# Roll of an 8192 x 8192 matrix by 100 columns: the heads' DMAs moved from GpSimd to SP and ACT

## The chip, the cores and the metric

The kernel runs on one core of one Trainium2 chip. The metric is the device time in microseconds (us). Before the change the median of 3 runs is 816.8 us (815.75 to 818.27). Nothing is multiplied here: the kernel moves data, and its work is done by the core's 16 DMA engines, which are fed by queues that SP, ACT and GpSimd (POOL in the profile) issue to. VectorE (DVE) makes a few small copies.

## The reference

```python
def setup_inputs():
    return {"x": np.random.randn(8192, 8192).astype(np.float32), "shift": 100}

def reference(x, shift):
    return np.roll(x, shift, axis=1)
```

Every row of 8192 floats (32 KB) is turned to the right by s = 100 floats: `out[r, c] = x[r, c - 100]`, and the last 100 floats of a row come to its front. All of x, 268.44 MB, must be read, and as much written.

## The kernel before

Each output row is cut at column a. `a` is 100 rounded up to 128 and then raised by another 128, so a = 256, and g = a - s = 156.

**The long pieces** are columns 256 to 8191 of each output row: 7936 floats, 31,744 bytes, copied from DRAM to DRAM. The rows are taken in 128 blocks of 64. A block is four DMAs (j = 0 to 3) of 16 rows each; SP issues j = 0 and 2, ACT j = 1 and 3, all in line 43. Each of the DMAs is 496 KB and puts one row on each of the 16 DMA engines. In the last four blocks every DMA is cut into two halves of 248 KB. The semaphores that the framework gives to DMAs of SP and ACT are eight, taken in turn, and a DMA waits until the last user of its semaphore has landed. So at most eight DMAs of SP and ACT together are under way. In the kernel before SP has four of the eight semaphores for itself and ACT the other four.

**The heads** are columns 0 to 255 of each output row (1 KB). They are made of two runs of the input: the last 100 floats of the row and its first 156. They go through SBUF, in 16 stages of 512 rows, four rows to a partition (Q = 4). A stage has

- line 72: one DMA that reads, for three of every four rows, the 256 floats that straddle the end of one row and the beginning of the next, into tile `t` (384 KB in runs of 1 KB)
- line 73: the last 100 floats of each fourth row, into `h` (50 KB in runs of 400 bytes), and line 76: the first 156 floats of each first row, into `h` (78 KB in runs of 624 bytes)
- lines 74 and 77: two VectorE copies from `t` to `h`, which swap the order of the two runs
- line 80: one DMA that stores `h` (512 KB, runs of 1 KB) into columns 0 to 255 of the 512 output rows

All 64 of these DMAs are issued by GpSimd: first the 48 loads of the 16 stages, then the 16 stores. Both pools have 16 buffers, so that no stage waits for a buffer. GpSimd's DMAs have eight semaphores of their own. SP and ACT never wait for the heads, and the heads never wait for the long pieces: they meet on the DMA engines alone, and GpSimd's loop over the stages is traced after the loop of the long pieces but runs beside it from the start.

Of the kernel before, what the change touches and what calls it, by code (L numbers as in the profile page):

```python
# [1 line left out]

# [4 lines left out]


@with_exitstack
def kernel(  # L10
    ctx: ExitStack,
    tc: tile.TileContext,
    x: bass.AP,
    shift: int,
    out: bass.AP,
):
    nc = tc.nc
    n_rows, n_cols = x.shape
    s = shift % n_cols
    a = -(-s // 128) * 128  # L20
    if 0 < a <= 384 and a + 128 <= n_cols:
        a += 128
    g = a - s
    P = nc.NUM_PARTITIONS
    engines = [nc.sync, nc.scalar]
    n_chunks = 16
    rows = n_rows // n_chunks

    xm = x.rearrange("(c e j) w -> c j e w", e=16, j=4)
    om = out.rearrange("(c e j) w -> c j e w", e=16, j=4)
    if a < n_cols:
        blocks = n_rows // 64
        mid = (a + n_cols) // 256 * 128
        for c in range(blocks):
            parts = ((a, mid), (mid, n_cols)) if c >= blocks - 4 and a < mid else ((a, n_cols),)  # L40
            for j in range(4):
                for lo, hi in parts:
                    engines[j % 2].dma_start(out=om[c, j, :, lo:hi], in_=xm[c, j, :, lo - s:hi - s])
    if a == 0:
        return


    if a > 512:
        for i in range(n_chunks):
            r = slice(i * rows, (i + 1) * rows)  # L50
            nc.gpsimd.dma_start(out=out[r, :s], in_=x[r, n_cols - s:])
            if g > 0:
                nc.gpsimd.dma_start(out=out[r, s:a], in_=x[r, :g])
        return

    Q = 4  # L60
    n_st = n_rows // (P * Q)
    reads = ctx.enter_context(tc.tile_pool(name="reads", bufs=n_st))
    heads = ctx.enter_context(tc.tile_pool(name="heads", bufs=n_st))
    xt = x.rearrange("(k p q) c -> k p q c", q=Q, p=P)
    ot = out.rearrange("(k p q) c -> k p q c", q=Q, p=P)
    tiles = []
    for k in range(n_st):
        t = reads.tile([P, Q - 1, a], x.dtype)
        h = heads.tile([P, Q, a], x.dtype)
        lead = bass.AP(tensor=x.tensor, offset=(k * P * Q + 1) * n_cols - s,  # L70
                       ap=[[Q * n_cols, P], [n_cols, Q - 1], [1, a]])
        nc.gpsimd.dma_start(out=t[:], in_=lead)  # L72
        nc.gpsimd.dma_start(out=h[:, Q - 1, :s], in_=xt[k, :, Q - 1, n_cols - s:])  # L73
        nc.vector.tensor_copy(h[:, :Q - 1, :s], t[:, :, :s])  # L74
        if g > 0:
            nc.gpsimd.dma_start(out=h[:, 0, s:], in_=xt[k, :, 0, :g])  # L76
            nc.vector.tensor_copy(h[:, 1:, s:], t[:, :, s:])  # L77
        tiles.append(h)
    for k, h in enumerate(tiles):
        nc.gpsimd.dma_start(out=ot[k, :, :, :a], in_=h[:])  # L80


# [1 line left out]
_INS = ['x', 'shift']  # L84
_OUTS = [((8192, 8192), 'float32')]

_NUMBERS = {'shift': 100}


# [26 lines left out]
```

## Time and profile before

| what | value |
|---|---|
| median of the runs | 816.8 us (815.75 to 818.27) |
| profiled execution, its own time: first to last instruction (span) | 828.0 us |
| bytes that the DMA engines moved | 276.90 MB, mean 334 GB/s |
| bytes read from HBM, and written to it | 268.44 MB each, 648 GB/s together |
| busy: VectorE, GpSimd | 12.3 us, 41.3 us |
| last issue of a head's store by GpSimd | 379.6 us |
| median from issue to landing: a long piece's DMA, a load of `t`, a store of `h` | 12.7 us, 50.6 us, 108.2 us |

The profiled execution is 11.2 us (1.4%) longer than the median of the runs. SP and ACT issue DMAs and do nothing else, so they have no busy time in the profile. A byte of a long piece is counted once in the bytes that the engines moved, and twice at HBM (it is read there and written there); a byte of a head is counted twice in the bytes moved (a load into SBUF and a store from it), and each of the two meets HBM once. The queue q0 is GpSimd's, in which software writes the descriptors; q1 and q10 are those of SP and ACT. "Share" of a queue is the time that its packets took, as a share of 16 engines over the span or the window.

### The profile page before, as it was taken

How to read it: one execution, taken by the hardware profiler on the slowest of the kernel's cores; microseconds unless marked ns; L12 is line 12 of the kernel's file. 1: busy time of each engine (PE TensorE's matmuls, PEld its weight loads, DVE VectorE, ACT ScalarE, POOL GpSimd, SP SyncE). 2: the span in 40 equal slices, each digit the busy share in tenths (PEclk: the TensorE clock that was granted, in tenths of full speed). 3: DMA queues.
4: the chain of work that ended last, by engine and by line, in shares of the span. 5: the costliest groups of instructions: out<-in, count | busy, mean ns of one | idle time of the engine just before them, and what ended most of it. 6: DMA issues, size and time to landing. Idle time of an engine off the chain costs nothing. (4 is left out here: it accounts for less than half of the span.)

```text
span 828.0 us, 689 instructions
## 1 busy us (share of the span) xinstructions
DVE 12.3 (1%) x32; POOL 41.3 (5%) x68
## 2 busy tenths in 40 slices
DVE  0000000000010000000000000000000000000000
POOL 2011000000021100000000000000000000000000
DMA  9999999999999999999999999999999999999998
GB/s 308 340 350 334 344 340 337 337 339 344 337 342 348 352 351 345 354 339 346 347 341 344 333 325 325 319 330 333 330 324 322 335 330 328 322 331 328 327 314 300
DMA packets 22278, 276.90 MB, mean 334 GB/s; under 512 B 9473, under 2 KB 9729, under 8 KB 13825
## 3 DMA queue, kind: packets, MB, share of 16 engines
q1 hardware_dynamic: 8448, 130.04, 46.1%
q10 hardware_dynamic: 8448, 130.04, 44.7%
q0 software_dynamic: 5376, 16.78, 8.4%
q14 instruction: 6, 0.04, 0.0%
HBM read 268.44 MB, written 268.44 MB: 648 GB/s over the span
## 5 line engine op out<-in xcount | busy, mean ns | idle before, releaser
L80 POOL DMA_DIRECT2D out_dram<-h x16 | 11.5, 724 | 126.6 <-DMA out_dram<-h 86.8
L76 POOL DMA_DIRECT2D h<-in_x_dram x16 | 8.7, 542 | 141.4 <-DMA t<-in_x_dram 141.4
L72 POOL DMA_DIRECT2D t<-in_x_dram x16 | 12.2, 762 | 30.8 <-DMA h<-in_x_dram 30.0
L73 POOL DMA_DIRECT2D h<-in_x_dram x16 | 8.9, 559 | 39.9 <-DMA h<-in_x_dram 39.9
L74 DVE COPY h<-t 128x300 f32<-128x300 f32 x16 | 6.1, 382 | 260.2 <-DMA t<-in_x_dram 260.2
L77 DVE COPY h<-t 128x468 f32<-128x468 f32 x16 | 7.5, 467 | 0.0
L97 POOL MEMSET const-float32-0.0<- 128x1 f32 x1 | 0.1, 99 | 0.2 <-issue 0.2
L97 POOL MEMSET const-bfloat16-1.0<- 128x1 bf16 x1 | 0.1, 102 | 0.0
L97 POOL MEMSET const-float32-1.0<- 128x1 f32 x1 | 0.1, 99 | 0.0
L97 POOL MEMSET const-uint8-127<- 128x1 uint8 x1 | 0.1, 99 | 0.0
## 6 DMA issues: line engine op xcount, KB each, us to landing
out_dram<-in_x_dram ACTq DMA_DIRECT2D x248, 496.0 KB, 12.7
out_dram<-in_x_dram SPq DMA_DIRECT2D x248, 496.0 KB, 12.7
out_dram<-h POOLq DMA_DIRECT2D x16, 512.0 KB, 108.2
t<-in_x_dram POOLq DMA_DIRECT2D x16, 384.0 KB, 50.6
out_dram<-in_x_dram SPq DMA_DIRECT2D x16, 248.0 KB, 6.0
out_dram<-in_x_dram ACTq DMA_DIRECT2D x16, 248.0 KB, 5.9
h<-in_x_dram POOLq DMA_DIRECT2D x16, 78.0 KB, 43.2
h<-in_x_dram POOLq DMA_DIRECT2D x16, 50.0 KB, 49.9
```

The source lines that it names most:

```text
L72: nc.gpsimd.dma_start(out=t[:], in_=lead)
L73: nc.gpsimd.dma_start(out=h[:, Q - 1, :s], in_=xt[k, :, Q - 1, n_cols - s:])
L74: nc.vector.tensor_copy(h[:, :Q - 1, :s], t[:, :, :s])
L76: nc.gpsimd.dma_start(out=h[:, 0, s:], in_=xt[k, :, 0, :g])
L77: nc.vector.tensor_copy(h[:, 1:, s:], t[:, :, s:])
L80: nc.gpsimd.dma_start(out=ot[k, :, :, :a], in_=h[:])
L97: nc = _bacc.Bacc("TRN2", target_bir_lowering=False, num_devices=1)
```

## The change

GpSimd issues no DMA any more. The heads' DMAs are put between the long pieces of SP and ACT. The loop over blocks `c` issues the four DMAs of a block (now in a helper, `copies`), and `step` is 128 // 17 = 7. After block 7k + 3 stage k is fetched: `t` by SP (line 66), the two small runs by ACT (lines 67 and 70), and the two VectorE copies follow (lines 68 and 71). After block 7k + 13, ten blocks later, stage k is stored, by SP for even k and by ACT for odd k (line 82). So the fetches follow blocks 3, 10, ... 108 and the stores blocks 13, 20, ... 118 of 128. The pools shrink from 16 buffers each to 3 for `t` and 4 for `h`. The eight semaphores of SP and ACT now also serve the heads' DMAs, in the order in which they are traced: a fetch takes three of them, a store one.

```diff
-    if a < n_cols:
-        blocks = n_rows // 64
-        mid = (a + n_cols) // 256 * 128
+    blocks = n_rows // 64
+    mid = (a + n_cols) // 256 * 128
+
+    def copies(c):
+
+        last = None
+        parts = ((a, mid), (mid, n_cols)) if c >= blocks - 4 and a < mid else ((a, n_cols),)
+        for j in range(4):
+            for lo, hi in parts:
+                if lo < hi:
+                    last = engines[j % 2].dma_start(out=om[c, j, :, lo:hi], in_=xm[c, j, :, lo - s:hi - s])
+        return last
...
-    reads = ctx.enter_context(tc.tile_pool(name="reads", bufs=n_st))
-    heads = ctx.enter_context(tc.tile_pool(name="heads", bufs=n_st))
...
-    tiles = []
-    for k in range(n_st):
+    reads = ctx.enter_context(tc.tile_pool(name="reads", bufs=3))
+    heads = ctx.enter_context(tc.tile_pool(name="heads", bufs=4))
+
+    def fetch(k):
         t = reads.tile([P, Q - 1, a], x.dtype)
         h = heads.tile([P, Q, a], x.dtype)
         lead = bass.AP(tensor=x.tensor, offset=(k * P * Q + 1) * n_cols - s,
                        ap=[[Q * n_cols, P], [n_cols, Q - 1], [1, a]])
-        nc.gpsimd.dma_start(out=t[:], in_=lead)
-        nc.gpsimd.dma_start(out=h[:, Q - 1, :s], in_=xt[k, :, Q - 1, n_cols - s:])
+        nc.sync.dma_start(out=t[:], in_=lead)
+        nc.scalar.dma_start(out=h[:, Q - 1, :s], in_=xt[k, :, Q - 1, n_cols - s:])
         nc.vector.tensor_copy(h[:, :Q - 1, :s], t[:, :, :s])
         if g > 0:
-            nc.gpsimd.dma_start(out=h[:, 0, s:], in_=xt[k, :, 0, :g])
+            nc.scalar.dma_start(out=h[:, 0, s:], in_=xt[k, :, 0, :g])
             nc.vector.tensor_copy(h[:, 1:, s:], t[:, :, s:])
-        tiles.append(h)
-    for k, h in enumerate(tiles):
-        nc.gpsimd.dma_start(out=ot[k, :, :, :a], in_=h[:])
+        return h
+
+    step = blocks // (n_st + 1)
+    held = []
+    for c in range(blocks):
+        copies(c)
+        if c % step == step // 2 and len(held) < n_st:
+            held.append(fetch(len(held)))
+        k = c // step - 1
+        if c % step == step - 1 and 0 <= k < n_st:
+            engines[k % 2].dma_start(out=ot[k, :, :, :a], in_=held[k][:])
```

More of the change, by code (lines that the diff above doesn't have):

```diff
@@ L35 @@
     om = out.rearrange("(c e j) w -> c j e w", e=16, j=4)
-    if a < n_cols:
-        blocks = n_rows // 64
-        mid = (a + n_cols) // 256 * 128
-        for c in range(blocks):
[L40 to L49, printed above, removed]
+    blocks = n_rows // 64
[8 more added lines that the diff above has]
+        return last
+    if a == 0 or a > 512:
+        for c in range(blocks):
+            copies(c)
+        for i in range(n_chunks if a else 0):
             r = slice(i * rows, (i + 1) * rows)
@@ L71 @@
                        ap=[[Q * n_cols, P], [n_cols, Q - 1], [1, a]])
-        nc.gpsimd.dma_start(out=t[:], in_=lead)
-        nc.gpsimd.dma_start(out=h[:, Q - 1, :s], in_=xt[k, :, Q - 1, n_cols - s:])
+        nc.sync.dma_start(out=t[:], in_=lead)
+        nc.scalar.dma_start(out=h[:, Q - 1, :s], in_=xt[k, :, Q - 1, n_cols - s:])
         nc.vector.tensor_copy(h[:, :Q - 1, :s], t[:, :, :s])
         if g > 0:
-            nc.gpsimd.dma_start(out=h[:, 0, s:], in_=xt[k, :, 0, :g])
+            nc.scalar.dma_start(out=h[:, 0, s:], in_=xt[k, :, 0, :g])
             nc.vector.tensor_copy(h[:, 1:, s:], t[:, :, s:])
-        tiles.append(h)
-    for k, h in enumerate(tiles):
-        nc.gpsimd.dma_start(out=ot[k, :, :, :a], in_=h[:])
+        return h
+    step = blocks // (n_st + 1)
+    held = []
+    for c in range(blocks):
+        copies(c)
+        if c % step == step // 2 and len(held) < n_st:
[3 more added lines that the diff above has]
+            engines[k % 2].dma_start(out=ot[k, :, :, :a], in_=held[k][:])
 _INS = ['x', 'shift']
```

## The prediction

> **What bounds the kernel now.** I read first the page's queue table, then the stretches of the span, then the queues inside two of these stretches, then the waits. The question is whether the DMA engines or the memory behind them set the pace, because the change leaves every byte as it is and alters only who carries the heads, in what packets and when.
>
> The queue table of the whole execution:
>
> ```profile
> q1 hardware_dynamic: 8448, 130.04, 46.1%
> q10 hardware_dynamic: 8448, 130.04, 44.7%
> q0 software_dynamic: 5376, 16.78, 8.4%
> HBM read 268.44 MB, written 268.44 MB: 648 GB/s over the span
> ```
>
> The shares add to 99.2%: the 16 engines hold a packet nearly all the time. The heads take 8.4% of 828.0 us, that is 69.6 us of every engine, for 6.1% of the bytes. That looks like an engine-bound kernel in which heads are dear. The stretches say otherwise (the columns after the window are its length, busy VectorE and GpSimd, clock, DMA share, GB/s):
>
> ```profile
> 120.00:180.00 60.00, 2.25 (x6) 6.06 (x10) 1.00 0.99 340
> 300.00:360.00 60.00, 0.00 (x0) 2.86 (x4) 1.00 1.01 350
> ...
> 540.00:600.00 60.00, 0.00 (x0) 0.00 (x0) 1.00 0.99 329
> 660.00:720.00 60.00, 0.00 (x0) 0.00 (x0) 1.00 1.00 326
> 800.00:828.00 28.00, 0.00 (x0) 0.00 (x0) 1.00 0.88 301
> ```
>
> Heads are loaded up to about 240 us and stored up to about 500 us; behind that only long pieces move, and the rate falls, from 340 to 350 down to 326 to 329 GB/s. The queues of three stretches (20 to 240, 240 to 480, 500 to 780 us) give the reason:
>
> ```profile
> DMA packets 6855, 74.83 MB, mean 340 GB/s; under 512 B 2782, under 2 KB 3001, under 8 KB 4719
> q0 software_dynamic: 2579, 7.04, 17.1%
> ```
>
> ```profile
> DMA packets 7247, 82.88 MB, mean 345 GB/s; under 512 B 2656, under 2 KB 2693, under 8 KB 4923
> q0 software_dynamic: 2611, 9.14, 11.7%
> ```
>
> ```profile
> DMA packets 5787, 91.83 MB, mean 328 GB/s; under 512 B 2893, under 2 KB 2893, under 8 KB 2893
> q1 hardware_dynamic: 2892, 45.94, 50.8%
> q10 hardware_dynamic: 2893, 45.88, 48.5%
> ```
>
> A long piece's byte meets HBM twice, a head's byte once per DMA. So HBM saw (2 x 74.83 - 7.04) / 220 us = 648 GB/s while heads were loaded, (2 x 82.88 - 9.14) / 240 = 653 while they were stored, and 2 x 91.83 / 280 = 656 with none. Three mixes, one rate within 1.2%. The long pieces themselves got quicker when the heads took engine time away from them: 82.3% of 16 x 220 us (q1 and q10, 40.2 and 42.1%) over 67.79 MB / 31,744 B = 2136 pieces is 1.36 us a piece beside the loads, 99.3% of 16 x 280 us over 2893 pieces is 1.54 us without heads. The fastest tenth of the packet records of a long piece is 1.175 us, 27.0 GB/s. So an engine has slack, and 328 / 27.0 = 12.1 engines at their best would carry what 16 carry now. HBM traffic at about 656 GB/s is the bound; 536.87 MB / 656 = 818 us of the 828 are that.
>
> The rest is small: 8 us, of which up to 220 x (1 - 648/656) + 240 x (1 - 653/656) = 3.8 us lie in the stretches with heads, some 2 us before the first packet, and 28 x (1 - 301/328) = 2.3 us in the tail.
>
> Lastly the waits, of the queues and of GpSimd:
>
> ```profile
> SPq L43 <- DMA out_dram<-in_x_dram: 680.3, 260, 4.9
> ```
>
> ```profile
> POOL h L76 <- DMA t<-in_x_dram: 141.4, 13, 14.6
> POOL out_dram L80 <- DMA out_dram<-h: 86.8, 7, 15.6
> ```
>
> SP waits 680 us for a landing before it may issue, so issue is never late. GpSimd's waits are off the path: its last store is issued at 379.6 us.
>
> **The change, part by part.** The sum is made against the profiled 828.0 us; the median of the runs is 816.8, 0.986 of it, and differences are carried over at that ratio.
>
> *GpSimd's 64 issues go* (41.3 us busy in all, 0.55 to 0.76 us each). Nothing waits for them at the end: 0.
>
> *Issues added to SP and ACT.* SP gets 16 loads of `t` and 8 stores, ACT 32 small loads and 8 stores. An issue on SP lasts 0.51 us, on ACT 0.52 (median of the instruction rows), so 12 and 21 us over the span; if the larger shapes take what GpSimd's did (0.72 to 0.76) it is 18 and 30. SP issues a long piece's DMA every 3.15 us. The cover is the 680 us of waiting: 0. Without it a fetch would delay ACT by 1 us, 16 us in all.
>
> *Waits.* A store waits for VectorE's copies of its stage. They were fetched ten blocks, 40 long DMAs of 1.55 us, about 62 us earlier; a landing of 13 to 16 us and two copies of 0.37 and 0.47 us leave over 40 us. Were it late, six to eight long pieces stand behind it on that queue, and, through the shared semaphores, the other queue stops eight DMAs later. A fetch needs its buffer of `h` free: the store of stage k - 4 was issued 18 blocks before, over 100 us: 0. The GpSimd ring could never hold up a long piece, so these are new risks, not new costs.
>
> *Window of eight.* Eight long DMAs under way are 8 x 1.55 = 12.4 us of work, which is the 12.4 us to landing in the last stretch. A fetch puts three heads' DMAs in the window: five long pieces, 7.8 us, and the heads' 1.5 to 3 us, so 9.3 at least. The 16 landings of one long DMA lie 5.7 us apart from first to last (the middle eight within 2.0, the widest tenth over 7.8), and from issue to first packet the trace's start shows 1.4 us, with 0.5 for the issue. 5.7 + 1.9 is under 9.3; in the widest tenth 7.8 + 1.9 exceeds it by 0.4 us for the foremost engine alone. Between 0 and 16 x 3 x 0.4 = 19 us (were each of the three DMAs to cost that to all engines); I take 0, since four engines can be idle with HBM still full.
>
> *The heads' packets.* GpSimd's ring packed runs into packets of about 4 KB: 4352 of them without the semaphore writes. The hardware rings show one packet per run for the long pieces; for 1 KB runs no row shows it, so there are from 4352 to 18,432 packets. Undisturbed, a 4096-byte packet takes 0.159 us, one of seven 624-byte runs 0.169, one of a single 624-byte run 0.032: some 8 ns per packet come on top of the run. So one-run packets are 46 ns (1 KB), 23 (400 B) and 32 (624 B). A fetch is 24, 8 and 8 of them on each engine, 1.54 us; a store 32, 1.47 us. Those are the low ends. The high ends are the rates of q0 under load: 7.04 MB / 16 in 17.1% of 220 us is 11.7 GB/s an engine for loads, and 20.3 for stores; 0.524 MB then takes 2.8 and 1.6 us, and 0.2 more for the extra packets: 3.0 and 1.8. Sixteen stages are 48 to 77 us of an engine, against 69.6 now. In engine time nearly nothing.
>
> *The bursts.* Here is the cost. Today heads trickle for 480 us and some engine always has a long piece to fill HBM. Now all 16 engines meet the same burst at nearly the same time. If they met it exactly together, HBM would be used at one side only: a fetch loses 1.54 - 0.8 to 3.0 - 0.8 us (0.524 MB at 656 GB/s is 0.8), a store 0.67 to 1.0, and 16 stages 23 to 51 us. If they are well spread it is 0. They are spread by the 5.7 us of the landings. Four engines pass per us in the middle, so a burst of 1.5 us holds six: ten at 27.0 x 2 and six at 22 GB/s are 674, still over 656: no loss. A load of 3.0 us holds eight or nine: 7.5 x 54 + 8.5 x 11.7 = 505, 23% short for about 2 us, 0.46 us a fetch, 7.4 in all. A further part overlaps because the other queue's long pieces alternate with the burst. I take 4 for the fetches, the middle of 0 and 7.4, and 1 for the stores, whose rows were hardly stretched.
>
> *What may be gained:* the 3.8 us of the stretches with heads, if they were the software ring's doing; if they are the head traffic's own, nothing. I take 0; both ends stay in the range.
>
> Sum: 828.0 + 5 = 833, and 816.8 + 5 x 0.986 = 822.
>
> **Two rules weighed.** The row first: long pieces of 1.36 us beside heads and 1.54 without, and a constant 648 to 656 GB/s at HBM. The Trainium skill, "HBM Reference", Bandwidth, says that a core streaming alone is bounded by its 16 DMA engines. By that rule engine time is what counts, and the sum would be 828.0 - 69.6 + 48 to 77, or 806 to 835; the row decides for HBM in this copy from DRAM to DRAM. The same page's ceiling of about 716 GB/s for the memory would leave the measured 656 at 92% of it. The second row: landings of one DMA are about 7 us apart early in the run and 3.2 to 3.7 us late in it. "DMA: Bandwidth & Descriptors", Latency and other measured facts, guesses that two engines lag because the software ring's descriptors share their port. That speaks for the change, but by the rule too the gain is capped by the 3.8 us. A tighter spread would also let the bursts coincide more.
>
> **The rivals.**
> 1. *Covered:* the spread hides the bursts and the time stays within 0.3% (2.5 us, about what a measurement of this kernel can tell from no change). For it: engines' slack of a quarter. Against: reads of heads were stretched to more than twice their best. 816.8 + 0 to 2 us.
> 2. *Faster:* the software ring was the loss. Its place is the 460 us with heads, its price 3.8 us by HBM rates (813 us), and up to 21 us (796) if engine time is the bound after all and a burst costs its low end. It decides if more than 2.5 of the 3.8 us return and bursts cost under 1. Against: 460 us at 99% of the best rate leave little.
> 3. *Much slower:* the bursts coincide, or the hardware rings carry 1 KB runs more slowly than q0's rows, or the window runs dry. Full coincidence at the low end is +23 us (839), at the high end +51 (867); the window alone up to +19 (836). For it: all engines get a burst from one DMA, and nothing in the trace shows how these rings take 1152 short runs a stage. Against: 9 us of queued long pieces.
> 4. That heads stay with GpSimd is excluded: the built program has no DMA on it.
>
> **How the numbers follow.** Modest loss (+3 to +12 us, own range 819.5 to 829): 0.40, point 822. Covered: 0.28. Much slower: 0.17. Faster: 0.15. Faster 0.15, same 0.28, slower 0.57. The range goes from 812, the end of the small gain, to 842, a little above full coincidence at the low end; outside it I leave the engine-bound gain (0.05) and the larger losses (0.10).
>
> **What would show it.** Right: HBM rate about 656 GB/s between bursts and dips in narrow slices at each fetch, deeper than at stores; SP and ACT with heads' packets of 1 KB; no idle wait on VectorE at the stores; DMA share near 1.0. Wrong, if the share falls below 0.97 around the fetches (the window), if heads' packets take over 100 ns (the rings), if the stores cost more than the fetches, or if the long pieces' 1.54 us fall without HBM traffic falling.

## The result and the profile after

The changed kernel takes 822.15 us (median of 6 runs, 821.18 to 827.67) where the kernel before takes 817.95 us on the same chip (6 runs, 815.75 to 819.06). The ratio is 1.0068, 95% interval 1.005 to 1.0086: slower by 0.7%. (The ratios are estimates over the runs of both kernels and not quotients of the medians, which would be 1.0051 here.) On another chip the same pair came out at 834.44 and 828.7 us, ratio 1.0081 (1.0059 to 1.0103). The forecast was 822.0 us with a range from 812 to 842, slower at 0.57. The sum was right. Its terms were not, as the experiments show. One execution of the whole study, of the wide form of the changed kernel, ran 1.7% above the fastest of its kernel, in a slower state, and is left out of its figures.

The chips have to be kept apart: the kernel before takes 817.95 us on the chip of the result and 826.8, 826.85 and 828.7 us on the three others of this study. A second profile of the kernel before has a span of 824.3 us beside its own time of 826.12: a span is about 2 us under the time of its execution. The first profile's 828.0 us therefore was hardly an execution on the chip with 816.8 us; it looks like one of the slower chips. Below, profiles are compared where the chips gave the kernel before nearly the same time: its second profile (chip with 826.8 us) and the second profile of the changed kernel (chip with 828.7 us).

The queue table of the changed kernel, first profile (packets, MB, share of 16 engines):

```profile
q1 hardware_dynamic: 19072, 140.53, 50.1%
q10 hardware_dynamic: 17280, 136.33, 48.5%
HBM read 268.44 MB, written 268.44 MB: 655 GB/s over the span
```

The software ring is gone and the two hardware rings carry its bytes: 36,352 packets instead of 22,272. They are one packet per run, as bounded: in the packet records the median 1 KB run lasts 46 ns, the 400-byte run 24 and the 624-byte run 32, the prediction's low ends (46, 23 and 32); some are stretched, and the mean of the 1 KB runs is 54 ns on SP's ring and 48 on ACT's.

The DMA issues of the same profile (count, KB each, median us from issue to landing):

```profile
out_dram<-in_x_dram SPq DMA_DIRECT2D x248, 496.0 KB, 11.3
out_dram<-in_x_dram ACTq DMA_DIRECT2D x248, 496.0 KB, 10.9
t<-in_x_dram SPq DMA_DIRECT2D x16, 384.0 KB, 9.2
out_dram<-h SPq DMA_DIRECT2D x8, 512.0 KB, 12.5
out_dram<-h ACTq DMA_DIRECT2D x8, 512.0 KB, 16.6
```

A load of `t` lands in 9.2 us where GpSimd's needed 50.6, a store in 12.5 to 16.6 where it needed 108.2. The heads themselves got much faster; nobody was waiting for them.

What the queues wait for, SP's issues of the same profile (us in total, times, longest):

```profile
SPq L41 <- DMA out_dram<-in_x_dram: 463.4, 183, 8.4
...
SPq L41 <- DMA out_dram<-h: 55.6, 8, 9.0
```

Before, SP's longest wait was 4.9 us, and only for long pieces. Now SP stands 7 us on average, and up to 9.0, behind each of eight stores before it may issue a long piece. All eight are ACT's stores: each store shifts the turn of the semaphores by one, and the place that an ACT store holds is the one that SP needs next. And this is what the engines do meanwhile, in stretches cut around one fetch (issued from 106.8 to 113.1 us), the store of ACT at 130.4 us and the next fetch (153.8 to 156.8 us); the last two columns are DMA share and GB/s:

```profile
106.00:114.00 8.00, 0.00 (x0) 0.00 (x0) 1.00 1.04 346
114.00:120.00 6.00, 0.00 (x0) 0.00 (x0) 1.00 0.91 318
120.00:124.00 4.00, 0.75 (x2) 0.00 (x0) 1.00 1.00 383
124.00:130.00 6.00, 0.00 (x0) 0.00 (x0) 1.00 1.04 323
130.00:136.00 6.00, 0.00 (x0) 0.00 (x0) 1.00 0.98 347
136.00:144.00 8.00, 0.00 (x0) 0.00 (x0) 1.00 0.99 365
144.00:150.00 6.00, 0.00 (x0) 0.00 (x0) 1.00 0.75 254
150.00:158.00 8.00, 0.00 (x0) 0.00 (x0) 1.00 1.01 373
158.00:164.00 6.00, 0.00 (x0) 0.00 (x0) 1.00 0.95 284
164.00:170.00 6.00, 0.75 (x2) 0.00 (x0) 1.00 1.02 391
```

(The busy VectorE of two rows are the copies of a stage.) A packet is counted whole in the stretch in which it starts, so a share can pass 1. Two kinds of dip are to be seen. At 144 to 150 us the share falls to 0.75: by the landings of the trace the store issued at 130.4 us reached the first engine's end at 134.7, the ninth's at 135.9 and the last one's only at 144.5 us, and SP, with a long piece that needs this store's semaphore, issued nothing between 139.2 and 144.5. Other engines ran out of work. At 158 to 164 us, where a fetch is carried, the engines are nearly all busy (0.95) and yet move 284 GB/s, about 490 at HBM: that is the burst, one-sided at HBM (a fetch only reads there, a long piece reads and writes). Behind each dip comes a stretch at 373 to 391 GB/s. The kernel before also has short stretches at up to 392 GB/s (5.5 us, in its second profile), but no dry ones.

The 0.75 is nearly the worst of this profile and not typical of it. With each packet spread evenly over its duration, a stretch of 6 us slid over the profile from 20 to 760 us is under a share of 0.9 in four places only, 2.7% of the time; the kernel before never falls under 0.94.

Where an engine's time went: the mean over the 16 engines of the packet records' durations, in us, of the second profiles of both kernels. "Rest" is the span without them.

| | span | long pieces | heads | semaphore writes | rest |
|---|---|---|---|---|---|
| kernel before, second profile | 824.3 | 743.0 | 68.6 | 5.4 | 7.4 |
| changed kernel, second profile | 831.7 | 755.5 | 58.8 | 5.6 | 11.7 |

The heads became 9.8 us cheaper for an engine, and the long pieces 12.5 us dearer; the memory did not get faster. The rest grew by 4.3 us. It is the least time for which an engine holds no packet: where packets of one engine overlap, it comes out too small. Of the 7.4 us between the two spans some 2 us can be the chips'.

### The profile page after: what moved, and what is told of

Same layout as the page of the kernel before. It is cut to its first block, busy times and chain, and to the rows that moved or that the text cites. A ratio compares the mean times of both kernels' runs of the same rounds, so it can differ in the third digit from the quotient of the medians.

```text
span 819.2 us, 707 instructions
## 1 busy us (share of the span) xinstructions
DVE 12.0 (1%) x32; POOL 0.2 (0%) x4
## 4 chain that ended last, share of the span: by engine, by line
DMA 86%; ACTq 0%; issue 0%; DVEq 0%; DVE 0%
DMA out_dram<-in_x_dram 72%; DMA out_dram<-h 14%; ACTq L41 0%; DVEq L113 0%; DVE h L68 0%; ACTq L82 0%
## 6 DMA issues: line engine op xcount, KB each, us to landing
out_dram<-h SPq DMA_DIRECT2D x8, 512.0 KB, 12.5
out_dram<-h ACTq DMA_DIRECT2D x8, 512.0 KB, 16.6
```

## The experiments

Three theories were set against each other, under the numbers that the expectations use (there is no theory 3). Theory 1 is the prediction's: all engines are in a burst of heads together and HBM is used at one side only. Theory 2 is what the prediction had priced at nothing: heads' DMAs take places in the window of eight, and engines run dry. Theory 4: the odd numbers of heads' DMAs make SP and ACT swap semaphores, which ties the queues together. All ratios are to the kernel before on the same chip.

**The kernel before again, and the long pieces alone.** The first has no edit. The second:

```diff
     for c in range(blocks):
         copies(c)
-    (all of the heads: pools, fetch, stores)
```

> The kernel before, unchanged, to have a second profile of it beside its own time: the first profile has a span of 828.0 us, longer than every timed run. All theories: ratio 1.000, within 0.2%. If 828.0 was an unlucky execution, its span is about 2 us under its own time (as in the changed kernel's profile, 819.2 and 821.2), so about 816 us, and the HBM rate of its stretches comes out near 658 GB/s where the first profile gave 648 to 656.

> The heads are left out (columns 0 to 255 are never written); only the long pieces run, in the order of both kernels. It gives the price of the heads in each kernel. If HBM traffic is the bound, the long pieces need 520.1 of 536.9 MB: 818 x 0.969 = 792 us, and the heads cost 26 us in the kernel before and 30 in the changed one. If the engines' time is the bound, the heads' 8.4% of the queue table are the price and this runs in about 750 us.

Measured: 826.48 against 826.8 us, ratio 1.0001 (0.9989 to 1.0014), and for the long pieces alone 798.24 us, 0.9656 (0.9642 to 0.9669). The span of 824.3 us stands 2 us under its own 826.12, as expected; that it is not 816 us is the chip. In the second profile HBM saw (2 x 75.45 - 7.50) / 220 = 652, (2 x 83.41 - 8.75) / 240 = 659 and 2 x 78.94 / 240 = 658 GB/s in the stretches with loads, with stores and without heads: flat again, within about 1%.

The long pieces' 0.9656 is close to 0.969, their share of the HBM traffic, and far from the 0.917 that engine time would give. So memory traffic is the bound, as read. The heads cost 28.6 us in the kernel before, where their bytes alone would be 26. So at most about 3 us were to be had from carrying them better. Without heads the long pieces run at the same pace as behind the heads in the kernel before (240 us, first row the long pieces alone, second the kernel before):

```profile
500.00:740.00 240.00, 0.00 (x0) 1.00 1.00 328
```

```profile
500.00:740.00 240.00, 0.00 (x0) 0.00 (x0) 1.00 1.00 329
```

The run also bears on the second rule that the prediction weighed. The landings of one DMA lie 5.3 (ACT) and 6.0 us (SP) apart on average in it, with no DMA on the software ring at all, so the spread of 5.7 us in the kernel before isn't the ring's. In the changed kernel it is 3.3 to 4.0 us.

**Places without bursts.** Heads as in the kernel before, and beside them

```diff
+    def tiny(engine, m):
+        d = small.tile([16, 16], x.dtype)
+        engine.dma_start(out=d[:], in_=marks[m, :, 1024:1040])
...
+        if c % step == step // 2 and held < n_st:
+            tiny(nc.sync, 4 * held)
+            tiny(nc.scalar, 4 * held + 1)
+            tiny(nc.scalar, 4 * held + 2)
...
+        if c % step == step - 1 and 0 <= k < n_st:
+            tiny(engines[k % 2], 4 * k + 3)
```

> The kernel before, with its heads on GpSimd, and 64 tiny DMAs (16 x 64 bytes, into tiles that nobody reads) on SP and ACT at the places where the changed kernel has its heads' DMAs. They take the same places in the window of eight and bring no burst. Theory 1 (bursts leave HBM one-sided while all engines are in them): no change, ratio 1.000 within 0.2%. Theory 2 (the heads' DMAs take places in the window of eight, and engines run dry): most of the 4.2 us of the changed kernel, 1.004 to 1.006.

Measured: 831.82 us, 1.0055 (1.0039 to 1.0071). Sixty-four DMAs of 1 KB, whose packets take 0.7 us of an engine in all, cost 0.55%, some 4.6 us. Theory 1 expected none of it. This is within the interval of the whole change. The issues show why so little data costs anything (KB each, median us from issue to landing):

```profile
d<-in_x_dram ACTq DMA_DIRECT2D x40, 1.0 KB, 7.3
d<-in_x_dram SPq DMA_DIRECT2D x24, 1.0 KB, 10.0
```

1 KB holds its place for 7 to 10 us, where a long piece's 496 KB holds it for 12.3. Behind the three tiny DMAs issued at 116.3 to 123.0 us engines do run dry (share and GB/s in the last columns; GpSimd's heads run beside):

```profile
116.00:122.00 6.00, 0.00 (x0) 0.00 (x0) 1.00 0.92 311
122.00:128.00 6.00, 0.75 (x2) 1.84 (x3) 1.00 0.80 269
128.00:134.00 6.00, 0.75 (x2) 1.83 (x3) 1.00 0.97 383
```

By the packet records that is the smaller part of the loss. Against the second profile of the kernel before, 8.3 us shorter on the same chip, an engine's rest is only 2.2 us longer (9.6 and 7.4); the long pieces take 9.0 us more (752.0 and 743.0) and the heads, the tiny DMAs included, 3.8 us less. So it is shown that the places cost, and not shown that they cost by idle engines alone.

**More places, semaphores not swapped.**

```diff
-            tiny(nc.sync, 4 * held)
-            tiny(nc.scalar, 4 * held + 1)
-            tiny(nc.scalar, 4 * held + 2)
+            for i in range(4):
+                tiny(engines[i % 2], 6 * held + i)
...
-            tiny(engines[k % 2], 4 * k + 3)
+            for i in range(2):
+                tiny(engines[i], 6 * k + 4 + i)
```

> As the run with tiny DMAs beside the old kernel, but with four of them at a fetch's place and two at a store's, SP and ACT in turn: 96 places taken instead of 64, while each queue keeps its own four of the eight semaphores throughout. With 64 (three and one) the two queues swap semaphores at each of the 32 places and wait for each other's long pieces there. Theory 2 (places in the window): more places, so 1.0055 or more, up to 1.008. Theory 4 (the swap of semaphores, which ties the two queues together, is what costs): 1.000, within 0.2%.

Measured: 833.0 us, 1.0082 (1.0054 to 1.0111). Theory 4 falls as the cause: the queues now wait for each other's DMAs only 8 times, by the trace, and with 64 places some 210 times, and the loss is no smaller. It is 1.5 times that of 64 places, as the places are, though the two intervals overlap. The stretch from 500 to 740 us, in which both kernels move only long pieces and tiny DMAs, first with 64 places and then with 96:

```profile
500.00:740.00 240.00, 0.00 (x0) 0.00 (x0) 1.00 1.00 326
```

```profile
500.00:740.00 240.00, 0.00 (x0) 0.00 (x0) 1.00 0.98 323
```

329, 326 and 323 GB/s with none, 64 and 96 places. With 96 the share falls by 0.02. With 64 the rate falls and the share does not: there the long packets themselves last longer. Why they should is not shown by these runs. In this stretch the landings of one DMA lie 2.6 us apart (median) with 64 places and 6.2 in the kernel before; whether engines that run more in step use HBM worse was not tried. Each of the two profiles is one execution, and both were the slowest of their six.

**The loads alone.**

```diff
-            engines[k % 2].dma_start(out=ot[k, :, :, :a], in_=held[k][:])
+            nc.gpsimd.dma_start(out=ot[k, :, :, :a], in_=held[k][:])
```

(and 16 buffers in both pools)

> The change's fetches alone: loads of the heads by SP and ACT at the changed kernel's places, stores by GpSimd as soon as VectorE has copied (both pools with 16 buffers). Theory 1 by the prediction's split (4 of 5 us are the fetches'): 1.005. Theory 2: 48 of the 64 places in the window remain, three at a time, so 1.004 to 1.006 as well. If the stores' bursts are what costs: 1.000 to 1.002.

Measured: 829.27 us, 1.0037 (1.0022 to 1.0052). About half of the loss comes with the fetches (0.37 of 0.68 to 0.81%), the rest with the stores. Forty-eight places at the price of the tiny ones would be 0.0055 x 48 / 64 = 0.0041. It fits, but the interval leaves room for the prediction's 1.005 too, so the time doesn't tell theories 1 and 2 apart. The profile, of a typical execution, speaks against idle engines here: the rest is 6.2 us (7.4 in the kernel before on the same chip), the heads take 51.4 us (68.6) and the long pieces 764.3 (743.0).

**Twice the work in a place.** Long DMAs of 32 rows, in both kernels; the last four blocks as they were.

```diff
+    xw = x.rearrange("(c e j r) w -> c j e r w", e=16, j=2, r=2)
+    ow = out.rearrange("(c e j r) w -> c j e r w", e=16, j=2, r=2)
...
-            for j in range(4):
+            for j in range(2):
+                engines[j].dma_start(out=ow[c, j, :, :, a:], in_=xw[c, j, :, :, a - s:n_cols - s])
```

> The kernel before with long DMAs of 32 rows (992 KB) but in the last four blocks, which stay as they are: the window of eight holds twice the work. It is the base for the next run. If HBM traffic alone is the bound: 1.000 within 0.3%. If the work in the window sets how well HBM is used: faster, 0.99 to 0.997.

> The changed kernel with long DMAs of 32 rows, as in the run before this one. Theory 2 (the window runs dry when heads take places in it): with twice the work per place the loss goes, and it is within 0.2% of that run. Theory 1 (bursts one-sided at HBM): the bursts are as large as ever, so it stays 0.5 to 0.7% slower than that run. Theory 4 (swap of semaphores): the swaps remain, with half as many long pieces to pass them, so 0.5% slower or more.

Measured: 835.05 us, 1.0107 (1.0088 to 1.0126), and 835.17 us, 1.0108 (1.0084 to 1.0131). With the doubled window the change costs nothing: 1.0108 / 1.0107 = 1.0001, some 0.3% either way by the two intervals. That is what theory 2 expected, on a base that got slower, which nobody expected. Where the base lost it: its landings lie 14 us apart from first to last (5.7 before), the end is ragged, and the rest of an engine's time rose from 7.4 to 12.4 us. The kernel before and the wide one, two stretches each (the last reaches beyond the ends, at 824.3 and 832.8 us; over the time that is there the shares are about 0.82 and 0.73, the rates 288 and 257 GB/s):

```profile
20.00:740.00 720.00, 12.03 (x32) 35.90 (x56) 1.00 1.00 339
...
800.00:840.00 40.00, 0.00 (x0) 0.00 (x0) 1.00 0.50 175
```

```profile
20.00:740.00 720.00, 12.03 (x32) 35.85 (x56) 1.00 1.00 337
...
800.00:840.00 40.00, 0.00 (x0) 0.00 (x0) 1.00 0.60 211
```

The rate in the body is 0.6% lower as well. In the wide form of the change the landings are 6 to 7 us apart, nearly twice the 3.5 of the narrow one, which would also spread the bursts over the engines. So the pair speaks for the window but doesn't exclude that bursts were hidden by the wider spread.

**Fewer places, longer bursts.** The counter-test, with the changed kernel run again on the same chip.

```diff
-    Q = 4
+    Q = 8      (the second run: Q = 16)
```

> The changed kernel, unchanged, on the chip of the next three, since chips differ by 1% (817.95 us and 826.8 us for the kernel before). All theories: 1.0068 within 0.2%. Its profile gives long pieces, heads and the rest to hold against the second profile of the kernel before (743.0, 68.6 and 7.4 us of an engine).

> The changed kernel with stages of 1024 rows (Q = 8): 8 fetches and 8 stores, half the places in the window (32), bursts twice as long (3 us of an engine for a store at 46 ns a run). Theory 2 (loss goes by places in the window): half the loss, 1.003 to 1.0035. Theory 1 (loss goes by one-sided bursts, which less and less fit into the spread of the engines): 1.007 or more, up to 1.015.

> The same with Q = 16: 4 stages, 16 places, bursts four times as long (6 us of an engine), longer than the 3.5 us that the landings lie apart. Theory 2: a quarter of the loss, 1.001 to 1.002. Theory 1: 4 x (5.5 + 5.9 - 2 x 3.2) = 20 us at full coincidence, so 1.01 to 1.025.

Measured: Q = 4 again 834.44 us, 1.0081 (1.0059 to 1.0103); Q = 8 836.3 us, 1.0098 (1.0081 to 1.0114); Q = 16 839.72 us, 1.013 (1.0113 to 1.0147). Here theory 2 alone falls: with a quarter of the places the loss grew from 0.81% to 1.30%. The longer holding of each place doesn't save it: count times median landing of the heads' DMAs add up to about 690, 410 and 240 us of one place. The burst costs when it is long. The parts of an engine's time agree: with Q = 16 the rest is back at 8.2 us (11.7 with Q = 4, 7.4 in the kernel before), while the long pieces take 768.4 us (755.5 and 743.0), although the heads' own packets take only 53.6. Engines are busy, and HBM moves less. The issues of Q = 16 show the burst's size (KB each, us to landing):

```profile
t<-in_x_dram SPq DMA_DIRECT2D x4, 1920.0 KB, 16.6
out_dram<-h SPq DMA_DIRECT2D x2, 2048.0 KB, 33.6
out_dram<-h ACTq DMA_DIRECT2D x2, 2048.0 KB, 19.2
```

If places cost 0.55% for 64 and in proportion, they are 0.55, 0.28 and 0.14% here, and the bursts what is left: 0.26, 0.70 and 1.16%, or 2, 6 and 10 us at 828.7 us. The sum of all bursts is nearly the same in the three; full coincidence was worked out as 23 us (20 for Q = 16). So a tenth of it is met with bursts of 1.5 us, a quarter with 3 us and 0.4 to 0.5 with 6 us, in order with landings that lie some 3.5 us apart. This split rests on the proportion and is an estimate. A real store also holds its place longer (12.5 to 16.6 us) than the tiny DMAs that set the price (7.3 to 10.0), so some of what is left may be the places' too.

**The stages split in more DMAs.** `t` in two loads, the store in two halves, once on both queues and once on one.

```diff
-        nc.sync.dma_start(out=t[:], in_=lead)
+        nc.sync.dma_start(out=t[:, :2], in_=lead2)
+        nc.sync.dma_start(out=t[:, 2:], in_=lead1)
...
-            engines[k % 2].dma_start(out=ot[k, :, :, :a], in_=held[k][:])
+            for i in range(2):
+                engines[i].dma_start(out=ot[k, :, 2 * i:2 * i + 2, :a], in_=held[k][:, 2 * i:2 * i + 2])
```

(in the second run `engines[k % 2]` in the last line; the two small loads, not shown, are issued one after each part of `t`)

> The changed kernel with the load of t in two DMAs (two runs and one run a partition) and each store in two halves, on SP and on ACT: a fetch is four DMAs, a store two, so that the queues keep their own semaphores between the places. Same bytes, same runs, same places. Theory 4 (swap of semaphores): 1.000 to 1.002 of the kernel before. Theory 2 (places): 96 places and not 64, so 1.007 to 1.010. Theory 1 (bursts leave HBM one-sided): the store's burst is halved on each ring but not on the engine, 1.006.

> The changed kernel with four DMAs a fetch and two a store, as in the run that came out at 1.0154, but with both halves of a store on the same queue: 96 places as there, while the other queue keeps long pieces beside the store. If that run's excess over the 1.0082 of 96 tiny DMAs came from both queues being in a store at once, this gives 1.008 to 1.010. If it came from the four-part fetch or from the places themselves, 1.0154 stays, within 0.3%.

Measured: 838.84 us, 1.0154 (1.0135 to 1.0173), and 842.12 us, 1.0158 (1.014 to 1.0175). More places cost more, in the direction of theory 2 and against theory 4. But the size is beyond all: 0.82% for 96 places and some 0.26% for the bursts make 1.1, and 0.5% are left over. They aren't from both queues being in a store at once, since they stay with one. Nor are they idle engines: the rest of an engine's time is 8.7 and 12.3 us, the long pieces 769.7 and 769.3. What lengthens them is open.

## Why the prediction was right, and where it was not

**The bound** was read rightly. HBM traffic and not engine time sets the pace: the long pieces alone run at 0.9656. The rival with the engine-bound gain (796 us), and the sum by the rule that a lone core is bounded by its engines (806 to 835), had the heads' 8.4% share as the thing to save; an engine did save 9.8 us of it and the time rose.

**The heads' packets** were right: 46, 23 to 24 and 32 ns, one packet per run, and 57 to 59 us of an engine for all heads, between the bounds of 48 and 77.

**Issues and waits** were right at nothing: SP's issue of a store lasts 0.59 us, of a load of `t` 0.37, and no store in either queue is held by VectorE's copies.

**The window of eight** is the term that failed. It was priced between 0 and 19 us and taken as 0, with the argument that four engines can be idle with HBM still full. The step looked at the foremost engine and at one fetch. What it missed is that a slow engine holds a head's place for the whole core: ACT's store at 130.4 us landed on the ninth engine at 135.9 and on the last at 144.5 us, and one queue issued nothing for 5 us. It stated the mark itself ("if the share falls below 0.97 around the fetches"); it fell to 0.91 behind the fetch shown and to 0.75 behind a store. Tiny DMAs in the same places cost 0.55%, 4.6 us: that is the size of most of the loss. How a place costs is open in part: with tiny DMAs the engines' rest grew by 2.2 of 8.3 us, in the changed kernel by 4.3 of 7.4, with the loads alone not at all; the remainder lies in long packets that last longer, beyond what the heads' packets gave back.

**The bursts** were priced at 5 us, between 0 and 51. They are there (284 GB/s at a share of 0.95), and they grow with their length, as the counter-test shows. At Q = 4 the estimate above leaves 2 us for them. They were split as 4 us for the fetches and 1 for the stores; the loads alone brought about half of the loss. The reasoning by the spread of the engines was of the right kind; its 3.0 us for a stretched load was high, as most runs keep 46 ns. It took 5.7 us for the spread, the kernel before's; in the changed kernel the landings lie some 3.5 us apart.

**What may be gained** (0 to 3.8 us, taken as 0): the heads of the kernel before cost 28.6 us, 3 more than their bytes. None of it came back.

**One reading** doesn't hold: that the landings of a DMA lie 3.2 to 3.7 us apart late in the run. In that trace they are 6.9 us apart at 20 to 240 us, 5.0 at 240 to 480 and 6.4 at 500 to 760 (medians); only the halved DMAs of the last four blocks come to about 2. The forecast didn't rest on it.

So 5 us were forecast from bursts and none from places, and 4 to 7 came, by the runs mostly from places. That the number came out is luck: an overpriced term stood in for one that was left out. A sum that is right is no proof of its terms.

## What to carry to other kernels

Where SP and ACT are limited to a fixed number of DMAs under way, a small DMA between large ones is charged a whole place until its slowest engine has landed, however few bytes it moves: here 7 to 10 us for 1 KB. A ring with semaphores of its own takes no such place; GpSimd's carried the heads here for at most about 3 us more than their bytes. Before one moves traffic to a faster path, one should ask who waits for it: here nobody did. And longer bursts cost more: with 2 and 4 times the burst the loss grew, so fewer and larger stages were no way out. That a burst is hidden while it is short against the spread of the engines fits these runs; it is not shown apart.

## What was not expected of the hardware

Behind a burst or a dry stretch the copy runs at 373 to 391 GB/s for some 4 to 8 us, about 770 GB/s at HBM at the most, where the steady long pieces hold 328 or 329 (about 657). The kernel before reaches 392 GB/s in 5.5 us as well. So the flat 652 to 659 GB/s of the kernel before is the steady pace of this traffic and not a ceiling for short times, and part of each dip is made up. Doubling the long DMAs to 992 KB made the kernel 1.07% slower (1.0088 to 1.0126), with landings 14 us apart instead of 5.7. And one kernel takes 817.95 us on one chip and 828.7 on another, more than what the change costs.
